# Layer A's score products on TensorE: pairs of fp32 products over 64 rows each, replaced by split fp32r products over 128 rows

## The chip, the cores and the metric

One core of one Trainium2 chip. The metric is the device time of one execution in microseconds (us), as the median of several runs; one more execution is taken by the hardware profiler.

## The reference

The program runs a token mixer block and then two more layers on 256 tokens of width 2048. The change lies in the first of these, layer A, a differential attention with 16 heads. Each head has two components of 64 channels, each with a query and a key that are normalised over those 64 channels, scores with a learned bias and a mask by chunks of 64 tokens, a softmax for each component, and the difference of the two as weights of the values:

```python
def _diff_attention(h, w_in, qk_g, lam_vecs, subln_g, w_out, rel_bias, layer_idx):
    ...
    q = _rmsnorm(q.reshape(B, S, H, 2, d), qk_g[0]) * (d ** -0.5)
    k = _rmsnorm(k.reshape(B, S, H, 2, d), qk_g[1])
    ...
        s = (jnp.einsum('bqhtd,bkhtd->bthqk', qblk, k).astype(jnp.float32)
             + jnp.transpose(bias, (2, 0, 1)).astype(jnp.float32))
        s = jnp.where(_chunk_mask(qpos, kpos), s, NEG_INF)
        p = jax.nn.softmax(s, axis=-1)
        attn = p[:, 0] - lam * p[:, 1]
        return jnp.einsum('bhqk,bkhe->bqhe', attn.astype(v.dtype), v)
```

Queries come in two blocks of 128 tokens; the first block sees 128 keys, the second 256. With 16 heads, 2 components and 2 blocks that makes 64 score products of 64 channels.

## The kernel before

Every large weight matrix is streamed from HBM in tiles of 512 KB. ScalarE (ACT) rounds each to fp32r, the format in which TensorE (PE) takes a product in one pass (`wh_...`), and VectorE (DVE) subtracts to get the rest (`wl_...`); activations are split in the same way, and three fp32r products (hi by hi, lo by hi, hi by lo) stand for one fp32 product. `gemm` does this. Its accumulators are called `acc_...`.

Layer A works in four groups of four heads (`layer_a`, i = 0 to 3). A group has three such gemms of 512 columns, `Aq`, `Ak` and `Av`, each of 96 products with 512 moving columns and eight weight tiles. `qk` normalises what Aq and Ak give, transposes it on PE (`pAq`, `pAk`), and moves it from PSUM to SBUF with one ACTIVATE for two heads (`TAq`, `TAk`: channels of component 0 in partitions 0 to 63, of component 1 in 64 to 127). `attention` then does, per head, the scores (tile `sA`, one PSUM bank per component), bias and minimum on DVE (`eA<-sA,biasA`), exponentials on ACT, the combination of both components on DVE (`eA<-eA,cfA,eA`), three transposes on PE (`ptA`), their eviction (`PTA`) and three products with the values (`poA`). The scores of heads 0 and 1 of a group are put out in one go, component 0 and 1 by turns; those of heads 2 and 3 per component, as banks come free:

```python
for c in range(2):
    cs = slice(64 * c, 64 * c + 64)
    mm(scores[g][c][:, cols], qT[cs, g, qs], kT[cs, g, ks], start=qs.start == 0, stop=True, skip_group_check=True)
```

Nothing is issued in the order of this code. Every operation is recorded (all have line 272, that of the recorder), and a list scheduler (`Plan.schedule`) writes out a fixed order for each engine from prices of its own (`Op.model`), priorities, and the rings of buffers that tiles take in turn (tags `t4`, `t2`, `ps`, `rps` and so on, with their counts in `BUFS`). So while a group's attention goes its way through DVE and ACT, PE does products of the next gemm (Aq of the next group, or Ag after the last) in between. SBUF tiles of 4 KB a partition, `TAq` and `TAk` among them, live in the ring `t4`. At run time the engines only wait for semaphores.

Of the kernel before, what the change touches and what calls it, by code (L numbers as in the profile page):

```python
# [10 lines left out]
F32 = mybir.dt.float32  # L11
F32R = mybir.dt.float32r
AF = mybir.ActivationFunctionType
OP = mybir.AluOpType
AX = mybir.AxisListType

T = 256
# [393 lines left out]
class Kernel:  # L411
# [156 lines left out]
    def run(self):  # L568
        tc, nc, a = self.tc, self.nc, self.a
        with ExitStack() as ctx:  # L570
# [18 lines left out]
            with tc.tile_pool(name="work2", bufs=1, reuse_waits="tile") as work:  # L589
                self.work = nc.pool(work, "work2", 1)  # L590
                self.BUFS = {"t1": 4, "t2": 9, "t15": 8, "t4": 14, "tiny": 24}
                self.layer_a()
                self.layer_b()
                nc.flush(tc)
# [659 lines left out]
    def layer_a(self):  # L1254
        nc, a = self.nc, self.a
# [10 lines left out]
        for i in range(4):  # L1266
            bias = self.sb(f"biasA{i}", [128, 4, 256], "t4")
            nc.sync.dma_start(bias, self.skewed(4 * i, 4))

            G.memset(bias[0:64, :, 0:64], -BIG)  # L1270
            qT = self.qk(f"Aq{i}", x, r, gq[:, 0:1])
            kT = self.qk(f"Ak{i}", x, r, gq[:, 1:2])
            acc = self.gemm(f"Av{i}", x)
            v = self.sb(f"vA{i}", [128, 2, 512], "t4")
            for t in range(2):
                S.activation(v[:, t], acc[t], AF.Identity, scale=r[:, t:t + 1])
            obs.append(self.attention(i, qT, kT, v, bias, nlam))
# [47 lines left out]
    def qk(self, group, x, r, gain):  # L1325
# [4 lines left out]
        out = self.sb(f"T{group}", [128, 4, T], "t4")  # L1330
# [10 lines left out]
        for hp in range(2):  # L1341
# [5 lines left out]
            S.activation(out[:, 2 * hp:2 * hp + 2], p, AF.Identity, scale=gain)  # L1347
        return out

    def attention(self, i, qT, kT, v, bias, nlam):  # L1350
# [5 lines left out]
        scores = {}  # L1356
        for h in range(4):
            n, st = f"{i}{h}", "r" * (h % 2)
            if h % 2 == 0:

                for g in (h, h + 1):
                    scores[g] = [self.ps(f"sA{i}{g}{c}", (128, 384), "r" * (g % 2)) for c in range(2)]
                    for cols, qs, ks in ((slice(0, 128), slice(0, 128), slice(0, 128)), (slice(128, 384), slice(128, 256), slice(0, 256))):
                        for c in range(2):
                            cs = slice(64 * c, 64 * c + 64)
                            mm(scores[g][c][:, cols], qT[cs, g, qs], kT[cs, g, ks], start=qs.start == 0, stop=True, skip_group_check=True)
            mn, sm = self.sb("mnA" + n, [128, 2, 2], "tiny"), self.sb("smA" + n, [128, 2, 2], "tiny")
            es = []
            for c in range(2):
                p = scores[h][c]  # L1370
# [267 lines left out]
```

## Time and profile before

| | |
|---|---|
| Runs | 1516.53 us median of 3 (1515.17 to 1516.99) |
| The profiled execution | 1517.89 us, its span on the core 1516.1 us |
| PE, its weight loads (PEld) | 98%, 88% of the span busy |
| DVE, ACT, POOL | 61%, 49%, 19% |
| DMA | 263.51 MB, all of it on hardware queues and instruction fetch |

The profile gives per instruction a start and a duration. Ends of matmuls are modelled, and matmuls overlap: what a product costs PE is read from one start to the next, not from its duration. A row of the timeline merges instructions of the same kind that follow each other (x16: sixteen records, the shape shown being the first one's), and names at its end what ended the idle time before it. `64*128` is the part of the array that the weights fill (rows by columns); the type shown for TensorE is f32 for fp32 and fp32r alike.

### The profile page before, as it was taken

How to read it: one execution, taken by the hardware profiler on the slowest of the kernel's cores; microseconds unless marked ns; L12 is line 12 of the kernel's file. 1: busy time of each engine (PE TensorE's matmuls, PEld its weight loads, DVE VectorE, ACT ScalarE, POOL GpSimd, SP SyncE). 2: the span in 40 equal slices, each digit the busy share in tenths (PEclk: the TensorE clock that was granted, in tenths of full speed). 3: DMA queues.
4: the chain of work that ended last, by engine and by line, in shares of the span. 5: the costliest groups of instructions: out<-in, count | busy, mean ns of one | idle time of the engine just before them, and what ended most of it. 6: DMA issues, size and time to landing. Idle time of an engine off the chain costs nothing. (4 is left out here: it accounts for less than half of the span.)

```text
span 1516.1 us, 25899 instructions
## 1 busy us (share of the span) xinstructions
PE 1481.7 (98%) x10201; PEld 1326.6 (88%) x10201; DVE 919.7 (61%) x1592; ACT 746.5 (49%) x1223; POOL 288.8 (19%) x390
## 2 busy tenths in 40 slices
PE   9999899899999999999999999999999999999999
PEld 8988789889979988777878787889999998988999
DVE  5875465375756765765656565666564458666544
ACT  6542354344455544756455555555443356455532
POOL 0139843812800000030303021100010001000000
PEclk9999999999999999999999999999999999999999
DMA  9645524444434467664545456556665554555563
GB/s 330 189 133 190 154 78 128 151 136 149 142 97 136 137 213 229 200 210 157 180 159 176 166 174 208 179 180 196 198 207 182 177 173 148 185 203 186 181 209 126
DMA packets 91962, 263.51 MB, mean 174 GB/s; under 512 B 19960, under 2 KB 26512, under 8 KB 91840
## 3 DMA queue, kind: packets, MB, share of 16 engines
q1 hardware_dynamic: 91840, 261.86, 54.2%
q8 instruction: 80, 1.31, 0.4%
q14 instruction: 42, 0.34, 0.1%
HBM read 253.92 MB, written 7.90 MB: 173 GB/s over the span
## 5 line engine op out<-in xcount | busy, mean ns | idle before, releaser
L272 POOL TENSOR_TENSOR blocks<-blocks,bt 32x30 f32<-32x30 f32 (+14 forms) x120 | 85.8, 715 | 9.4
L272 POOL TENSOR_TENSOR bt<-blocks 32x30 f32<-32x30 f32 (+14 forms) x120 | 77.6, 647 | 9.2
L272 PE MATMUL acc_rk<-xh,wh_rk 128*128 128x256 f32 x256 | 73.6, 289 | 1.0 <-ACT wh_rk L272 1.0
L272 PE MATMUL acc_rk<-xh,wl_rk 128*128 128x256 f32 x256 | 73.8, 289 | 0.5 <-DVE wl_rk L272 0.5
L272 PE MATMUL acc_rk<-xl,wh_rk 128*128 128x256 f32 x256 | 73.1, 286 | 0.0
L272 PE MATMUL acc_Ao<-mAh,wl_Ao 128*128 128x256 f32 x256 | 72.7, 284 | 0.0
L272 PE MATMUL acc_Bo<-mBh,wl_Bo 128*128 128x256 f32 x256 | 72.6, 284 | 0.0
L272 PE MATMUL acc_Ao<-mAh,wh_Ao 128*128 128x256 f32 x256 | 72.5, 283 | 0.0
L272 PE MATMUL acc_Ao<-mAl,wh_Ao 128*128 128x256 f32 x256 | 72.4, 283 | 0.0
L272 PE MATMUL acc_Bo<-mBl,wh_Bo 128*128 128x256 f32 x256 | 72.4, 283 | 0.0
L272 PE MATMUL acc_Bo<-mBh,wh_Bo 128*128 128x256 f32 x256 | 72.3, 283 | 0.0
L272 DVE TENSOR_TENSOR wl_Bo<-wr_Bo,wh_Bo 128x1024 fp32r<-128x1024 f32 x32 | 39.2, 1225 | 44.9 <-ACT wh_Bo L272 44.9
L272 DVE TENSOR_TENSOR wl_rk<-wr_rk,wh_rk 128x1024 fp32r<-128x1024 f32 (+1 forms) x33 | 41.2, 1247 | 40.3 <-ACT wh_rk L272 40.3
L272 DVE TENSOR_TENSOR wl_Av<-wr_Av,wh_Av 128x1024 fp32r<-128x1024 f32 x32 | 39.2, 1224 | 41.9 <-ACT wh_Av L272 41.8
L272 DVE TENSOR_TENSOR wl_Ao<-wr_Ao,wh_Ao 128x1024 fp32r<-128x1024 f32 x32 | 41.3, 1292 | 36.2 <-ACT wh_Ao L272 36.2
L272 DVE TENSOR_TENSOR wl_o<-wr_o,wh_o 128x1024 fp32r<-128x1024 f32 x32 | 39.2, 1225 | 38.1 <-ACT wh_o L272 38.1
L272 DVE TENSOR_TENSOR wl_Bg<-wr_Bg,wh_Bg 128x1024 fp32r<-128x1024 f32 x32 | 39.2, 1225 | 34.5 <-ACT wh_Bg L272 34.5
L272 ACT ACTIVATE wh_Bo<-wr_Bo 128x1024 fp32r<-128x1024 f32 x32 | 33.9, 1058 | 53.1 <-PE acc_Bo L272 49.8
L272 DVE TENSOR_TENSOR wl_Ag<-wr_Ag,wh_Ag 128x1024 fp32r<-128x1024 f32 x32 | 39.2, 1225 | 30.6 <-ACT wh_Ag L272 30.5
L272 PE MATMUL acc_Bv<-wl_Bv,xBh 128*128 128x412 f32 (+1 forms) x160 | 56.4, 353 | 1.0 <-DVE wl_Bv L272 1.0
L272 DVE TENSOR_TENSOR wl_Bv<-wr_Bv,wh_Bv 128x824 fp32r<-128x824 f32 (+1 forms) x40 | 40.6, 1019 | 26.8 <-ACT wh_Bv L272 26.6
L272 ACT ACTIVATE wh_rk<-wr_rk 128x1024 fp32r<-128x1024 f32 (+1 forms) x33 | 34.1, 1033 | 45.8 <-PE acc_rk L272 22.9
(764 smaller groups left out, 5376.1 us busy)
## 6 DMA issues: line engine op xcount, KB each, us to landing
wr_o<-w SPq DMA_DIRECT2D x32, 512.0 KB, 4.3
wr_Aq<-w SPq DMA_DIRECT2D x32, 512.0 KB, 3.6
wr_Ak<-w SPq DMA_DIRECT2D x32, 512.0 KB, 3.5
wr_Av<-w SPq DMA_DIRECT2D x32, 512.0 KB, 3.8
wr_Ag<-w SPq DMA_DIRECT2D x32, 512.0 KB, 3.5
wr_Ao<-w SPq DMA_DIRECT2D x32, 512.0 KB, 4.2
wr_Bg<-w SPq DMA_DIRECT2D x32, 512.0 KB, 3.3
wr_Bo<-w SPq DMA_DIRECT2D x32, 512.0 KB, 3.3
```

Source lines behind the costliest of these rows:

```text
L272: op.issued = getattr(getattr(self.nc, op.eng), op.method)(*op.args, **op.kw)
```

## The change

`qk` now stores each component by itself, in fp32r and over all 128 rows. For queries, rows 0 to 63 hold hi and rows 64 to 127 lo. For keys there are two tiles: one with hi in both halves, one with lo in rows 0 to 63 and zeros below. A score is then the sum of two fp32r products over 128 rows: hi by hi plus lo by hi, and hi by lo (with zeros under it). The products of a component stand in a row, and each reads the same 128 weight columns again. Per group ACT has 12 evictions of 64 partitions and 512 elements where it had 4 of 128 partitions, DVE 8 subtractions that it did not have, and POOL two memsets of 64x1024. The ring `t4` goes from 14 to 18 buffers, and `dynamic_dma_scratch_size` is set to 1024 bytes.

```diff
--- before.py
+++ after.py
@@ -588,7 +588,7 @@
                 nc.flush(tc)
             with tc.tile_pool(name="work2", bufs=1, reuse_waits="tile") as work:
                 self.work = nc.pool(work, "work2", 1)
-                self.BUFS = {"t1": 4, "t2": 9, "t15": 8, "t4": 14, "tiny": 24}
+                self.BUFS = {"t1": 4, "t2": 9, "t15": 8, "t4": 18, "tiny": 24}
                 self.layer_a()
                 self.layer_b()
                 nc.flush(tc)
@@ -1268,8 +1268,8 @@
             nc.sync.dma_start(bias, self.skewed(4 * i, 4))
 
             G.memset(bias[0:64, :, 0:64], -BIG)
-            qT = self.qk(f"Aq{i}", x, r, gq[:, 0:1])
-            kT = self.qk(f"Ak{i}", x, r, gq[:, 1:2])
+            qT = self.qk(f"Aq{i}", x, r, gq[:, 0:1], False)
+            kT = self.qk(f"Ak{i}", x, r, gq[:, 1:2], True)
             acc = self.gemm(f"Av{i}", x)
             v = self.sb(f"vA{i}", [128, 2, 512], "t4")
             for t in range(2):
@@ -1322,12 +1322,16 @@
                 blocks[b].append(z[:, 128 * b:128 * b + 128])
         self.split_tokens(mix, k0, blocks, scales)
 
-    def qk(self, group, x, r, gain):
+    def qk(self, group, x, r, gain, keys):
+
 
         nc = self.nc
         V, G, S = nc.vector, nc.gpsimd, nc.scalar
         acc = self.accs.pop(group, None) or self.gemm(group, x)
-        out = self.sb(f"T{group}", [128, 4, T], "t4")
+        out = [[self.sb(f"T{group}{hp}{i}", [128, 2, 2, T], "t4", F32R) for i in range(1 + keys)] for hp in range(2)]
+        if keys:
+            for _, lo in out:
+                G.memset(lo.bitcast(F32)[64:128], 0.0)
         z = [self.sb(f"z{group}{t}", [128, 8, 64], "t2") for t in range(2)]
         ss = self.sb(f"s{group}", [128, 2, 8], "tiny", bufs=None)
         for t in range(2):
@@ -1344,7 +1348,13 @@
                 for t in range(2):
                     h = 2 * hp + j
                     nc.tensor.transpose(p[:, j, t * 128:(t + 1) * 128], z[t][:, 2 * h:2 * h + 2].rearrange("p a b -> p (a b)"), self.ident)
-            S.activation(out[:, 2 * hp:2 * hp + 2], p, AF.Identity, scale=gain)
+            for c in range(2):
+                cs = slice(64 * c, 64 * c + 64)
+                hi, lo = out[hp][0][:, :, c], out[hp][1][0:64, :, c] if keys else out[hp][0][64:128, :, c]
+                S.activation(hi[0:64], p[cs], AF.Identity, scale=gain[cs])
+                if keys:
+                    S.activation(hi[64:128], p[cs], AF.Identity, scale=gain[cs])
+                V.scalar_tensor_tensor(lo, p[cs], gain[0:64], hi.bitcast(F32)[0:64], op0=OP.mult, op1=OP.subtract)
         return out
 
     def attention(self, i, qT, kT, v, bias, nlam):
@@ -1353,21 +1363,16 @@
         mm, tr = nc.tensor.matmul, nc.tensor.transpose
         V, G, S = nc.vector, nc.gpsimd, nc.scalar
         ob = self.sb(f"ob{i}", [128, 2, 512], "t4")
-        scores = {}
         for h in range(4):
             n, st = f"{i}{h}", "r" * (h % 2)
-            if h % 2 == 0:
-
-                for g in (h, h + 1):
-                    scores[g] = [self.ps(f"sA{i}{g}{c}", (128, 384), "r" * (g % 2)) for c in range(2)]
-                    for cols, qs, ks in ((slice(0, 128), slice(0, 128), slice(0, 128)), (slice(128, 384), slice(128, 256), slice(0, 256))):
-                        for c in range(2):
-                            cs = slice(64 * c, 64 * c + 64)
-                            mm(scores[g][c][:, cols], qT[cs, g, qs], kT[cs, g, ks], start=qs.start == 0, stop=True, skip_group_check=True)
             mn, sm = self.sb("mnA" + n, [128, 2, 2], "tiny"), self.sb("smA" + n, [128, 2, 2], "tiny")
             es = []
             for c in range(2):
-                p = scores[h][c]
+                p = self.ps(f"sA{n}{c}", (128, 384), st)
+                q, ks = qT[h // 2][0][:, h % 2, c], [k[:, h % 2, c] for k in kT[h // 2]]
+                for cols, t, m in ((slice(0, 128), 0, 128), (slice(128, 384), 1, 256)):
+                    for j, k in enumerate(ks):
+                        mm(p[:, cols], q[:, 128 * t:128 * t + 128], k[:, 0:m], start=t == j == 0, stop=j == 1, skip_group_check=True)
                 e = self.sb(f"eA{n}{c}", [128, 384], "t15")
                 for t, cols, b in ((0, slice(0, 128), self.keys(bias, h, 128, 128)), (1, slice(128, 384), self.keys(bias, h, 0, 256))):
                     V.tensor_tensor_reduce(e[:, cols], p[:, cols], b, -1.0, 3e38, op0=OP.add, op1=OP.min, accum_out=mn[:, c, t:t + 1])
@@ -1627,7 +1632,7 @@
     import concourse.bacc as bacc
     from concourse.bass_utils import run_bass_kernel_spmd
 
-    nc = bacc.Bacc("TRN2", target_bir_lowering=False, num_devices=1)
+    nc = bacc.Bacc("TRN2", target_bir_lowering=False, num_devices=1, dynamic_dma_scratch_size=1024)
     sent = arrays(inputs)
     a = {n: nc.dram_tensor(n, v.shape, mybir.dt.from_np(v.dtype), kind="ExternalInput").ap() for n, v in sent.items()}
     a["out"] = nc.dram_tensor("out", (D, T), F32, kind="ExternalOutput").ap()
```

The order on PE at the first scores of group 0. Names are sA, group, head, component; TAk and TAq with the group (before) or the group, pair of heads and hi or lo (after). Before:

```order
L272 MATMUL acc_Av0_1_7537<-wh_Av0_14_7560,xAl0_1252 128x512
L272 MATMUL sA000_7564<-TAk0_7526,TAq0_7493 128x128
L272 MATMUL sA001_7565<-TAk0_7526,TAq0_7493 128x128
L272 MATMUL sA000_7564<-TAk0_7526,TAq0_7493 128x256
L272 MATMUL sA001_7565<-TAk0_7526,TAq0_7493 128x256
L272 MATMUL sA010_7566<-TAk0_7526,TAq0_7493 128x128
L272 MATMUL sA011_7567<-TAk0_7526,TAq0_7493 128x128
L272 MATMUL sA010_7566<-TAk0_7526,TAq0_7493 128x256
L272 MATMUL sA011_7567<-TAk0_7526,TAq0_7493 128x256
L272 MATMUL acc_Aq1_0_7614<-wh_Aq1_0_7617,xAh0_1251 128x512
```

And now (head 0; the eight products of head 1 follow in the same way, then the same gemm row):

```order
L272 MATMUL acc_Av0_1_7541<-wh_Av0_14_7564,xAl0_1252 128x512
L272 MATMUL sA000_7570<-TAk000_7527,TAq000_7493 128x128
L272 MATMUL sA000_7570<-TAk001_7528,TAq000_7493 128x128
L272 MATMUL sA000_7570<-TAk000_7527,TAq000_7493 128x256
L272 MATMUL sA000_7570<-TAk001_7528,TAq000_7493 128x256
L272 MATMUL sA001_7572<-TAk000_7527,TAq000_7493 128x128
L272 MATMUL sA001_7572<-TAk001_7528,TAq000_7493 128x128
L272 MATMUL sA001_7572<-TAk000_7527,TAq000_7493 128x256
L272 MATMUL sA001_7572<-TAk001_7528,TAq000_7493 128x256
```

Eight fp32 products of heads 0 and 1, components by turns, have become sixteen, component after component. The later heads have two rows per component before, four now, at nearly the same places among the gemm's products.

On PE, the first transposes (ptA) of head 0 among products of the next gemm. Before, and now:

```order
L272 MATMUL acc_Aq1_1_7615<-wh_Aq1_0_7617,xAh0_1251 128x512
L272 MATMUL acc_Aq1_1_7615<-wl_Aq1_0_7618,xAh0_1251 128x512
L272 MATMUL ptA00_7574<-cst_73,eA000_7570 128x128
L272 MATMUL acc_Aq1_1_7615<-wh_Aq1_0_7617,xAl0_1252 128x512
L272 MATMUL ptA00_7574<-cst_73,eA000_7570 128x128 x2
L272 MATMUL acc_Aq1_0_7614<-wh_Aq1_2_7620,xAh0_1251 128x512
```

```order
L272 MATMUL acc_Aq1_0_7618<-wl_Aq1_2_7625,xAh0_1251 128x512
L272 MATMUL acc_Aq1_0_7618<-wh_Aq1_2_7624,xAl0_1252 128x512
L272 MATMUL ptA00_7576<-cst_73,eA000_7571 128x128
L272 MATMUL acc_Aq1_1_7619<-wh_Aq1_2_7624,xAh0_1251 128x512
L272 MATMUL ptA00_7576<-cst_73,eA000_7571 128x128 x2
L272 MATMUL acc_Aq1_1_7619<-wl_Aq1_2_7625,xAh0_1251 128x512
```

Between the last score of head 1 and the first transpose stood 11 gemm products; now there are 15.

On ACT, the eviction of the keys (TAk<-pAk) among the splits of weight tiles, late in gemm Av of group 0. Before, and now:

```order
L272 ACTIVATE wh_Av0_12_7557<-wr_Av0_12_7556 128x1024
L272 ACTIVATE TAk0_7526<-pAk00_7534,gq_7487 128x512
L272 ACTIVATE TAk0_7526<-pAk01_7535,gq_7487 128x512
L272 ACTIVATE wh_Av0_14_7560<-wr_Av0_14_7559 128x1024
L272 ACTIVATE wh_Aq1_0_7617<-wr_Aq1_0_7616 128x1024
L272 ACTIVATE wh_Aq1_2_7620<-wr_Aq1_2_7619 128x1024
```

```order
L272 ACTIVATE wh_Av0_12_7561<-wr_Av0_12_7560 128x1024
L272 ACTIVATE TAk000_7527<-pAk00_7538,gq_7487 64x2x256 x3
L272 ACTIVATE wh_Av0_14_7564<-wr_Av0_14_7563 128x1024
L272 ACTIVATE TAk000_7527<-pAk00_7538,gq_7487 64x2x256
L272 ACTIVATE TAk010_7529<-pAk01_7539,gq_7487 64x2x256 x2
L272 ACTIVATE wh_Aq1_0_7621<-wr_Aq1_0_7620 128x1024
L272 ACTIVATE TAk010_7529<-pAk01_7539,gq_7487 64x2x256 x2
L272 ACTIVATE wh_Aq1_2_7624<-wr_Aq1_2_7623 128x1024
```

On DVE at the same place, before, and now:

```order
L272 TENSOR_TENSOR wl_Av0_12_7558<-wr_Av0_12_7556,wh_Av0_12_7557 128x1024
L272 TENSOR_TENSOR wl_Av0_14_7561<-wr_Av0_14_7559,wh_Av0_14_7560 128x1024
L272 TENSOR_TENSOR wl_Aq1_0_7618<-wr_Aq1_0_7616,wh_Aq1_0_7617 128x1024
L272 TENSOR_TENSOR wl_Aq1_2_7621<-wr_Aq1_2_7619,wh_Aq1_2_7620 128x1024
L272 ISA eA000_7570,mnA00_7568<-sA000_7564,biasA0_7492 128x128
```

```order
L272 TENSOR_TENSOR wl_Av0_12_7562<-wr_Av0_12_7560,wh_Av0_12_7561 128x1024
L272 SCALAR_TENSOR_TENSOR TAk001_7528<-pAk00_7538,gq_7487,TAk000_7527 64x2x256 x2
L272 TENSOR_TENSOR wl_Av0_14_7565<-wr_Av0_14_7563,wh_Av0_14_7564 128x1024
L272 SCALAR_TENSOR_TENSOR TAk011_7530<-pAk01_7539,gq_7487,TAk010_7529 64x2x256
L272 TENSOR_TENSOR wl_Aq1_0_7622<-wr_Aq1_0_7620,wh_Aq1_0_7621 128x1024
L272 SCALAR_TENSOR_TENSOR TAk011_7530<-pAk01_7539,gq_7487,TAk010_7529 64x2x256
L272 TENSOR_TENSOR wl_Aq1_2_7625<-wr_Aq1_2_7623,wh_Aq1_2_7624 128x1024
L272 ISA eA000_7571,mnA00_7568<-sA000_7570,biasA0_7492 128x128
```

Three evictions stand ahead of the split of the last Av tile (wh_Av0_14) where two did, and two subtractions ahead of its second half (wl_Av0_14) where none did. On POOL the two memsets of a group stand ahead of the squares of its keys (qAk). The order of DMA issues on SP is the same as before, and so is the order of PE outside layer A.

## Rows read from the trace of the kernel before

**Rows 1.** The page: busy time by engine, granted clock by slice, the chain that ended last.

```profile
PE 1481.7 (98%) x10201; PEld 1326.6 (88%) x10201; DVE 919.7 (61%) x1592; ACT 746.5 (49%) x1223; POOL 288.8 (19%) x390
...
PEclk9999999999999999999999999999999999999999
...
PE 36%; DVE 1%; ACT 1%; POOL 0%; DMA 0%; issue 0%; ACTq 0%; DVEq 0%
PE acc_Bo L272 6%; PE acc_Ao L272 6%; PE acc_Ag L272 6%; PE acc_Bg L272 6%; PE acc_Bv L272 5%; PE acc_Bq L272 3%; PE acc_Bk L272 3%; PE pB L272 0%; PE tp L272 0%; PE poB L272 0%; POOL k L272 0%; PE sA L272 0%; DMA wr_Bv<-w 0%; PE poA L272 0%; ACT wh_Bv L272 0%
```

**Rows 2.** One stretch of layer A: us, busy us (instructions) by engine, clock, DMA, GB/s.

```profile
760.00:830.00 70.00, 69.89 (x340) 56.00 (x339) 42.77 (x82) 38.95 (x74) 11.18 (x8) 1.00 0.52 167
```

**Rows 3.** What works on tile sA: records, ns min/median/max, first and last start, forms.

```profile
L272 PE MATMUL sA<-TAk,TAq x128: 269/374/378, 697.4 to 945.9; 64*128 64x128 f32 x64, 64*128 64x256 f32 x64
```

**Rows 4.** Timeline, PE, group 0, first scores: start us, us, engine, what, records.

```profile
697.08 0.39 PE L272 MATMUL acc_Av<-wh_Av,xAl 128*128 128x512 f32 x1
697.40 1.58 PE L272 MATMUL sA<-TAk,TAq 64*128 64x128 f32 x16
698.91 0.50 PE L272 MATMUL acc_Aq<-wh_Aq,xAh 128*128 128x512 f32 x1
...
699.49 0.39 PE L272 MATMUL acc_Aq<-wh_Aq,xAl 128*128 128x512 f32 x1
```

**Rows 5.** Timeline, PE, group 0, a later head: a short run of scores.

```profile
712.08 0.39 PE L272 MATMUL acc_Aq<-wh_Aq,xAh 128*128 128x512 f32 x1
712.40 0.92 PE L272 MATMUL sA<-TAk,TAq 64*128 64x128 f32 x4
713.25 0.50 PE L272 MATMUL acc_Aq<-wl_Aq,xAh 128*128 128x512 f32 x1
...
713.82 0.40 PE L272 MATMUL acc_Aq<-wh_Aq,xAh 128*128 128x512 f32 x1
```

**Rows 6.** Timeline, PE, acc_Bk: first and last of 36 starts, fp32r, 256 columns.

```profile
1199.80 0.28 PE L272 MATMUL acc_Bk<-xBh,wh_Bk 128*128 128x256 f32 x1
...
1204.00 0.28 PE L272 MATMUL acc_Bk<-xBh,wl_Bk 128*128 128x256 f32 x1
```

**Rows 7.** Timeline, PE, pn: eight records of two moving columns, 128-column weights.

```profile
327.04 1.05 PE L272 MATMUL pn<-cst,sq 128*128 128x2 f32 x8
327.96 0.36 PE L272 MATMUL acc_za<-xh,wh_za 128*128 128x256 f32 x1
```

**Rows 8.** Timeline, group 0: transposes of head 0, with what they waited for.

```profile
701.31 0.39 PE L272 MATMUL acc_Aq<-wl_Aq,xAh 128*128 128x512 f32 x1
...
701.80 0.14 PEld L272 LDWEIGHTS ptA<-cst,eA 128*128 128x128 f32 x1 [0.53 <-DVE eA L272]
...
702.71 0.39 PE L272 MATMUL acc_Aq<-wl_Aq,xAh 128*128 128x512 f32 x1
```

**Rows 9.** Timeline, PE, group 0: first and last start around another head's three transposes.

```profile
714.51 0.39 PE L272 MATMUL acc_Aq<-wh_Aq,xAh 128*128 128x512 f32 x1
...
715.77 0.40 PE L272 MATMUL acc_Aq<-wl_Aq,xAh 128*128 128x512 f32 x1
```

**Rows 10.** Timeline, all engines, late acc_Av of group 0.

```profile
687.85 1.27 ACT L272 ACTIVATE TAk<-pAk,gq 128x512 f32<-128x512 f32 x2 [1.09 <-PE pAk L272]
...
689.33 1.06 ACT L272 ACTIVATE wh_Av<-wr_Av 128x1024 fp32r<-128x1024 f32 x1 [0.21 <-PE acc_Av L272]
...
690.42 1.22 DVE L272 TENSOR_TENSOR wl_Av<-wr_Av,wh_Av 128x1024 fp32r<-128x1024 f32 x1 [2.41 <-ACT wh_Av L272]
...
694.59 0.39 PE L272 MATMUL acc_Av<-wh_Av,xAh 128*128 128x512 f32 x1
```

**Rows 11.** Groups on DVE by form: count | busy us, mean ns of one | idle before.

```profile
L272 DVE SCALAR_TENSOR_TENSOR xAl<-tp,par,xAh 128x256 fp32r<-128x256 f32 x12 | 5.7, 479 | 0.8 <-ACT xAT L272 0.7
L272 DVE SCALAR_TENSOR_TENSOR xAl<-tp,par,xAh 128x128 fp32r<-128x128 f32 x8 | 2.7, 347 | 0.1
```

## The prediction, written before the changed kernel ran

> **What bounds the kernel now.** First the page: PE is busy for 98% of the span, the granted clock is in its top tenth in all 40 slices, and the chain that ended last runs through PE and its gemms, with DVE and ACT at 1% each [rows 1]. Then the stretches of layer A: from 760 to 830 us PE is busy for 69.89 of 70 us at clock 1.00 (2.4 GHz), while DVE has 42.77 us of work and ACT 38.95 [rows 2]. So here the time is the sum of what PE's instructions take from one start to the next, as long as nothing that it needs comes late. Next, what works on the score tile: 64 products stand in 128 records, two for each fp32 product [rows 3]. Last, the timeline of PE around the scores, to price them with their surroundings.
>
> A gemm product of 512 columns is the measure there: from 694.59 [rows 10] to 697.08 [rows 4] are 11 starts, 0.226 us each.
>
> **What goes.** In group 0 the sixteen records of heads 0 and 1 stand between two gemm products. From 697.08 to 699.49 are 2.41 us with three gemm starts; less 3 x 0.226 = 0.68 the scores cost 1.73 us [rows 4]. A short run of four records, one component of a later head: 712.08 to 713.82, 1.74 us, again three gemm starts, so 1.06 us [rows 5]. A group has one long run and four short ones, 1.73 + 4 x 1.06 = 5.97 us, and four groups 23.9 us. I take the other three groups at the same price: their forms and counts are the same.
>
> The two kinds of run differ. From the first score to the next gemm product a short run takes 0.85 us [rows 5], the long run 1.51 us for four times the records [rows 4]: its components, in the two halves of the array's rows, run beside each other. In the short runs there is nothing to run beside.
>
> **What comes.** 128 fp32r products over all rows, 64 with 256 moving columns, 64 with 128. 256 columns: from 1199.80 to 1204.00 are 35 intervals, 0.120 us each [rows 6]. An fp32r product with 128 moving columns is not in the trace. From below: 256 columns more cost 0.226 - 0.120 = 0.106 us, so 128 fewer would take 0.053 off, 0.067 us. From above: were it taken in four passes, 4 x 128 columns, it would be as long as 512 columns, 0.226 us. I take 0.115 us, from the row that is nearest in the weights: eight records that each load 128 columns and then stream only two take 327.04 to 327.96, 0.92 us, 0.115 each [rows 7]. Those weights are fp32, but the new products load just as many columns for each record. A group then costs 16 x 0.115 + 16 x 0.120 = 3.76 us, four groups 15.0 us. Saved: 23.9 - 15.0 = **8.8 us**; 11.9 us at 0.067 (a group 2.99), 1.7 us at 0.226 (a group 5.54).
>
> Here a rule speaks against the change. The Trainium skill (TensorEngine Tiling (Array Packing), Key Properties) has tiles of the array work independently, each loading weights and multiplying in parallel; a contraction over 64 rows could so run two by two. By the rule alone every head would cost half a long run, 2 x 1.73 = 3.46 us a group, and the change would lose 4 x 0.30 = 1.2 us. The trace bears it out in the long run and not in the short ones, which hold half the heads at 4.24 us a group; the measured runs decide, and the sum keeps 8.8 us.
>
> **A wait that goes with it.** The first transposes of head 0 wait 0.53 us for DVE's `eA` [rows 8]. From 701.31 to 702.71 are 1.40 us with three gemm starts (0.68), so three transposes took 0.72 us; another head's, not waited for, took 1.26 us less four gemm starts (0.90), 0.36 us [rows 9]. The difference, 0.36 us, occurs once a group: 1.4 us. In the new order 15 gemm products stand ahead of them instead of 11, four more times 0.226 = 0.9 us, and the long run itself costs 16 x 0.1175 = 1.88 us, not 1.73. The chain of DVE and ACT up to `eA` keeps its operations, and the first half of component 0 is now done after two records. So the transposes come about 1 us later relative to a chain that starts no later, and I count the wait as gone. If it stays: 0.
>
> **What lies beside other work.** Per group ACT has 8 more evictions. Two of today's take 1.27 us [rows 10], 0.64 each; with half the partitions, but the same 512 elements in each, I take the same: 5.1 us a group. DVE has 8 more subtractions from PSUM; such an instruction takes 347 ns for 128 columns and 479 for 256 [rows 11], 132 per 128 columns, so 743 ns for 512, 5.9 us a group. In 70 us of layer A, less than a group takes, DVE has 27 us free and ACT 31 [rows 2]: there is room, and what matters is what stands behind it in order. The tightest place is the last tile of Av. Today its first half is split on ACT at 689.33, its second on DVE at 690.42, and its first product starts at 694.59 [rows 10]. Now three evictions stand ahead: 687.85 + 3 x 0.64 = 689.77, the split ends at 690.83; on DVE the subtraction that needs the third eviction ends at 690.5, and the second half runs from about 690.9 to 692.1. That leaves 2.5 us. Behind it the tiles of Aq are split about 1 us later than today, one gemm tile (12 x 0.226 = 2.7 us) or more ahead of need. The keys of heads 0 and 1 are ready by 692, the scores want them at 697.4. So this costs nothing; were that cover gone, each us beyond 2.5 would be paid in all four groups.
>
> Edits at nothing: the memsets on POOL (8 in all, ahead of squares on an engine at 11.18 of 70 us [rows 2]); four more buffers in `t4`; the scratch size. DMA issues keep their order. Past layer A nothing changes its order.
>
> **Sum.** 8.8 + 1.4 = 10.2 us. From the profiled execution's 1517.89 us that gives 1507.7; the median of the runs shown is 1.36 us below it, so for a median 1516.53 - 10.2 = **1506.3 us**.
>
> **Rivals.**
> 1. *The weight load hides.* If 128 columns cost 0.067 us, the saving is 11.9 + 1.4 = 13.3 us, 1503.2. For it: 256 and 512 columns lie on one line with a small offset, so no weight load shows yet at 0.120. Against it: 0.115 with two columns [rows 7]. Chance 0.11. The Trainium skill (TensorE: Matmul & The Clock Gate, Back-to-back issue gap) gives about 81 ns for a sustained pair of weight load and product of 128 columns; by that, an estimate, a group would take 3.22 us and the kernel about 1504.1 us. No row here shows such a pair below 0.115.
> 2. *The change doesn't do what it says.* With 128 moving columns fp32r goes no faster than four passes, 0.226 us: 1.7 + 1.4 = 3.1 us, 1513.4. For it: nothing in the trace has fp32r below 256 columns, and half of the new products are such. Against it: nothing shows a step in the price from 512 to 256. Chance 0.15.
> 3. *The keys come in the way, and it gets slower.* ACT and DVE run in order, and the evictions of `TAk` stand ahead of `wh_Av`, `wl_Av`. If the half-partition forms that move between halves cost k times my prices, the last tile of Av is ready at 687.85 + (3 x 0.64 + 0.74) k + 1.3; it is late beyond k = 2.05 and costs 2.66 (k - 2.05) a group. From k = 3.3 that eats all 10.2 us and 3 more; at k = 4 it is 20.8 us in four groups, 1527.1. For it: neither form is in the trace. Against it: a factor of 3 on a form that keeps its 512 elements per partition. Chance of slower 0.04, of a part of the gain eaten 0.06.
>
> **How the numbers follow.** The forecast has 0.64. About 0.2% (3 us) is what a measurement can tell from no change. Faster by more: the forecast, rival 1, half of the part eaten (0.03) and a third of rival 2, which lies on that bound (0.05), 0.83. Within 0.2%: the rest of rival 2 and of the part eaten, 0.13. Slower: 0.04. The range takes in rival 1 less half the spread of the runs (1503.2 - 0.9 = 1502.3), and upwards the forecast with the wait kept and 0.13 us for each new product (saved 4 x (5.97 - 4.16) = 7.2, 1509.3) plus the whole spread, 1.8: 1511.1. Rival 2 and the slower case, 0.19, lie outside.
>
> **What would show it.** In the new profile: score records one after another about 0.117 us apart, sixteen of them from the last Av product to the first of the next gemm in 2.1 us (1.88 and one gemm start); four in about 0.47 us; no idle "issue" at either end; no DVE wait ahead of head 0's transposes; layer A shorter by 2.5 us a group. Wrong it would be if 128-column records stood 0.22 us apart, or if `acc_Av` or `acc_Aq` waited for `wh` or `wl` behind `TAk`.

## The result, and the profile after the change

The changed kernel takes 1505.56 us (median of 5 runs, 1504.8 to 1510.02), the kernel before 1516.53 (now 5 runs, 1515.17 to 1516.99): a ratio of 0.9938, with an interval of 0.992 to 0.9955. Forecast were 1506.3 us, with 1502.3 to 1511.1 as the range.

The page has the same shape as before [rows 1]: PE is busy for 98% of the span, and DVE and ACT have more to do.

```profile
PE 1471.5 (98%) x10201; PEld 1329.8 (88%) x10201; DVE 942.3 (63%) x1624; ACT 767.8 (51%) x1255; POOL 296.0 (20%) x398
```

The windows view from 760 to 830 us, against [rows 2]: PE has no idle time left, DVE went from 42.77 to 49.07 us and ACT from 38.95 to 46.11. The added work is there, and PE does not feel it.

```profile
760.00:830.00 70.00, 70.00 (x352) 58.84 (x350) 49.07 (x92) 46.11 (x84) 16.58 (x12) 1.00 0.55 174
```

The timeline of PE in group 0 (start, length, operation): the long run, a short run, and head 0's transposes, against [rows 4], [rows 5] and [rows 8].

```profile
695.19 0.39 PE L272 MATMUL acc_Av<-wh_Av,xAl 128*128 128x512 f32 x1
695.42 2.00 PE L272 MATMUL sA<-TAk,TAq 128*128 128x128 f32 x16
697.26 0.40 PE L272 MATMUL acc_Aq<-wh_Aq,xAh 128*128 128x512 f32 x1
...
700.44 0.40 PE L272 MATMUL acc_Aq<-wh_Aq,xAl 128*128 128x512 f32 x1
700.67 0.27 PE L272 MATMUL ptA<-cst,eA 128*128 128x128 f32 x1
700.70 0.48 PE L272 MATMUL acc_Aq<-wh_Aq,xAh 128*128 128x512 f32 x1
701.01 0.38 PE L272 MATMUL ptA<-cst,eA 128*128 128x128 f32 x2
701.15 0.48 PE L272 MATMUL acc_Aq<-wl_Aq,xAh 128*128 128x512 f32 x1
701.47 0.40 PE L272 MATMUL acc_Aq<-wh_Aq,xAl 128*128 128x512 f32 x1
...
704.45 0.39 PE L272 MATMUL acc_Aq<-wl_Aq,xAh 128*128 128x512 f32 x1
704.67 0.62 PE L272 MATMUL sA<-TAk,TAq 128*128 128x128 f32 x4
705.13 0.40 PE L272 MATMUL acc_Aq<-wh_Aq,xAl 128*128 128x512 f32 x1
```

Sixteen products from 695.19 to 697.26: 2.07 us, less one gemm start (0.226) 1.84, or 0.115 each, the mean of eight products with 128 and eight with 256 moving columns. Four from 704.45 to 705.13: 0.68, less 0.226 is 0.45. The first score follows an Av product by 0.23 us, an ordinary distance; before, it was 0.32. The transposes: 700.44 to 701.47, 1.03 less three gemm starts (0.68), 0.35 us, and no wait in brackets.

To compare kernels I use one stretch throughout: from the last Av product of group 0 to the first product of `acc_Ao`, so all scores of layer A and nothing behind it. Before, it runs from 697.08 to 1030.8, **333.7 us**; now from 695.19 to 1019.0, **323.8 us**. That is 9.9 us. What PE's weight loads waited for in it, before (first fence) and now (second; columns: engine, what waited, releaser, us in total, times, longest):

```profile
PEld acc_Aq L272 <- issue: 4.0, 12, 0.3
PEld sA L272 <- issue: 2.9, 8, 0.4
PEld ptA L272 <- DVE eA L272: 2.1, 4, 0.5
PEld sA L272 <- ACT eA L272: 1.5, 4, 0.4
PEld ptA L272 <- issue: 1.3, 4, 0.3
PEld acc_Ag L272 <- issue: 1.3, 4, 0.3
```

```profile
PEld tp L272 <- issue: 0.4, 1, 0.4
```

13.1 us of waits became 0.4. They overlap with PE's work in part, so they aren't all gain. The waits for issue of 0.3 to 0.4 us stand on both sides of the score runs: on entering the 64-row form (`sA`) and on leaving it (`acc_Aq`, `acc_Ag`, `ptA`).

The two profiled executions differ by 12.3 us, 1517.89 to 1505.56. The stretch has 9.9 of it; 1.9 lie ahead, where PE's order is the same in both kernels (697.08 against 695.19 for the same Av product), and 0.5 behind. Whether the 1.9 belong to the change, experiment 7 shows.

### The profile page after: what moved, and what is told of

It is laid out like the page before. It is cut to its first block, busy times and chain, and to the rows that moved or that the text cites. A ratio compares the mean times of both kernels' runs of the same rounds, so it can differ in the third digit from the quotient of the medians.

```text
span 1503.8 us, 25983 instructions
## 1 busy us (share of the span) xinstructions
PE 1471.5 (98%) x10201; PEld 1329.8 (88%) x10201; DVE 942.3 (63%) x1624; ACT 767.8 (51%) x1255; POOL 296.0 (20%) x398
## 4 chain that ended last, share of the span: by engine, by line
PE 86%; POOL 6%; DVE 3%; issue 2%; DMA 1%; ACT 1%; SPq 0%; ACTq 0%; DVEq 0%; POOLq 0%
PE acc_Bo L272 6%; PE acc_Ao L272 6%; PE acc_o L272 6%; PE acc_Ag L272 6%; PE acc_Av L272 6%; PE acc_Aq L272 6%; PE acc_Bg L272 6%; PE acc_Ak L272 5%; PE acc_Bv L272 5%; PE acc_rk L272 3%; PE acc_zb L272 3%; PE acc_q L272 3%; PE acc_Bq L272 3%; PE acc_Bk L272 3%; POOL bt L272 3%; PE acc_v L272 3%
## 5 line engine op out<-in xcount | busy, mean ns | idle before, releaser
L272 POOL TENSOR_TENSOR blocks<-blocks,bt 32x30 f32<-32x30 f32 (+14 forms) x120 | 81.8, 682 | 9.4
L272 POOL TENSOR_TENSOR bt<-blocks 32x30 f32<-32x30 f32 (+14 forms) x120 | 80.8, 674 | 9.2
L272 ACT ACTIVATE wh_Ao<-wr_Ao 128x1024 fp32r<-128x1024 f32 x32 | 33.8, 1057 | 45.5 <-PE acc_Ao L272 38.7
L272 ACT ACTIVATE wh_o<-wr_o 128x1024 fp32r<-128x1024 f32 x32 | 33.9, 1060 | 45.1 <-PE acc_o L272 37.6
```

The costliest lines, as they stand in the source:

```text
L272: op.issued = getattr(getattr(self.nc, op.eng), op.method)(*op.args, **op.kw)
```

## The experiments

All were timed beside the kernel before on their own chip, so each ratio is with that.

**1. The 64-row form alone.** fp32 as before, but over all 128 rows, with zeros in the half of the key tile that the component doesn't use; the ring `t4` and the scratch size are those of the change:

```diff
-        out = self.sb(f"T{group}", [128, 4, T], "t4")
+        out = [self.sb(f"T{group}{c}", [128, 4, T], "t4") for c in range(1 + keys)]
+        if keys:
+            G.memset(out[0][64:128], 0.0)
+            G.memset(out[1][0:64], 0.0)
...
-                            mm(scores[g][c][:, cols], qT[cs, g, qs], kT[cs, g, ks], start=qs.start == 0, stop=True, skip_group_check=True)
+                            mm(scores[g][c][:, cols], qT[0][:, g, qs], kT[c][:, g, ks], start=qs.start == 0, stop=True, skip_group_check=True)
```

> The kernel before, with one key tile per component whose other 64 rows are zero, so that a score is an fp32 product over all 128 rows: four passes as before, no two halves of the array. Theory (the short runs lose their 0.42 us on top of their passes with the 64-row form, the long run loses its overlap): 0.226 us for 128 columns and 0.44 for 256, so a long run 2.66 us instead of 1.73, a short one 0.67 instead of 1.06, a group 5.3 instead of 5.97, four groups 2.6 us less; and the wait of head 0's transposes goes, since the long run is 0.9 us longer: 1.4 us. From the last product of Av in group 0 to the first of Ao (333.7 us before) 329.7; total about 1512.5. Rival (the fixed 0.42 us comes with any run of small products, not with the 64-row form): a group 2.66 + 4 x 0.67 + 5 x 0.42 = 7.4 us, 5.9 us more, total about 1521.

Measured: 1515.14 us (median of 12) against 1518.15, ratio 0.998 (0.9968 to 0.9992). The stretch is 1026.7 - 696.86 = 329.8 us. In it the trace has no wait of PE's loads at all. PE around the long run:

```profile
696.86 0.39 PE L272 MATMUL acc_Av<-wh_Av,xAl 128*128 128x512 f32 x1
697.09 2.78 PE L272 MATMUL sA<-TAk,TAq 128*128 128x128 f32 x16
699.52 0.58 PE L272 MATMUL acc_Aq<-wh_Aq,xAh 128*128 128x512 f32 x1
699.94 0.40 PE L272 MATMUL acc_Aq<-wl_Aq,xAh 128*128 128x512 f32 x1
700.17 0.39 PE L272 MATMUL acc_Aq<-wh_Aq,xAl 128*128 128x512 f32 x1
```

The gemm product behind the run also takes longer than 0.226 us here, so I count three gemm starts, as in [rows 4]: from 696.86 to 700.17 are 3.31 us, less 0.68 is 2.63, 0.165 per record. That is dearer than the 1.73 us of the pairs, since nothing runs beside anything now. A short run, counted in the same way, takes 0.67 us where it took 1.06 (711.28 to 712.63, less three gemm starts). Both are the theory's prices (2.66 and 0.67), and the stretch is 3.9 us shorter, 329.8 against the theory's 329.7. So 2.4 of the 9.9 us come from giving up the 64-row form, its idle ends and its pairs together, with everything still fp32; 1.5 come with the wait of head 0's transposes, which goes here too; the other 6 come with fp32r in place of fp32.

**2. Moving columns.** The changed kernel with 256 moving columns in every score product, 128 of them computed in vain for the first query tile:

```diff
-                for cols, t, m in ((slice(0, 128), 0, 128), (slice(128, 384), 1, 256)):
+                for cols, t, m in ((slice(256, 512), 0, 256), (slice(0, 256), 1, 256)):
```

> The changed kernel, with 256 moving columns in all 128 score products (the first query block takes 128 keys that nothing reads). Theory (a product of 128 moving columns is bound by the load of its 128 weight columns): 64 products go from 0.115 to 0.120 us, 0.3 us more than the changed kernel: from the last Av product to the first of Ao 324.1 us (323.8 there), total about 1506. Rival (the stream sets it, 0.067 us for 128 columns): 64 x 0.053 = 3.4 us more, 327.2 us, about 1509.

Measured: 1507.52 us (6 runs), ratio 0.9934 (0.9915 to 0.9953). The stretch is 1022.6 - 698.08 = 324.5, 0.7 us more than the change. The long run stands between gemm products at 698.08 and 700.22, 2.14 us: (2.14 - 0.226) / 16 = 0.120 each. Only half of its products have changed, so a product with 128 moving columns costs 2 x 0.115 - 0.120 = 0.110 us, and the 128 columns more are worth about 0.01 us (0.7 us over the 64 products), twice the theory's 0.005 and far below the rival's 0.053: the moving side is not what a product takes most of its time from.

**3. Pairs in fp32.** The kernel before, with the scores of heads 2 and 3 also put out for both components by turns, and the transposes `ptA` 0.9 us later in PE's order so that none falls between:

```diff
+        if op.method == "transpose" and op.args[0].tensor.name.startswith("ptA"):
+            return d.end + self.LATENCY[d.eng][op.eng] + self.MARGIN + 900
...
-                            mm(scores[g][c][:, cols], qT[cs, g, qs], kT[cs, g, ks], start=qs.start == 0, stop=True, skip_group_check=True)
+                            op = mm(scores[g][c][:, cols], qT[cs, g, qs], kT[cs, g, ks], start=qs.start == 0, stop=True, skip_group_check=True)
+                            if h == 2:
+                                op.deps[freed[g % 2]] = "data"
```

> The kernel before, fp32 over 64 rows as it was, but the scores of heads 2 and 3 are put out with both components in turns, as those of heads 0 and 1 are (the scheduler is told to wait until both banks are free), and the transposes of the weights are placed 0.9 us later. Theory (components in the two halves of the rows overlap wherever they stand together): a head of a short run costs 1.06 us once, not twice; 2.1 us a group, 8.5 us in all, and 1.4 us for the wait of the transposes: 323.8 us from the last Av product to the first of Ao, total about 1506.6, as the changed kernel. Rival (only the fixed cost is shared, the passes don't overlap): a head 1.28 + 0.42 = 1.70 us, 3.4 us in all and 1.4: 328.9 us, about 1511.7.

Measured: 1509.53 us (6 runs), ratio 0.9941 (0.9925 to 0.9956). The stretch is 326.8 us, between theory and rival. A pair run:

```profile
712.86 0.39 PE L274 MATMUL acc_Aq<-wh_Aq,xAh 128*128 128x512 f32 x1
713.18 0.93 PE L274 MATMUL sA<-TAk,TAq 64*128 64x128 f32 x8
714.04 0.50 PE L274 MATMUL acc_Aq<-wl_Aq,xAh 128*128 128x512 f32 x1
```

Eight records take 0.86 us from the first start to the next gemm product, where four took 0.85 [rows 5]: the second component is free. The waits show where most of the missing 3 us went: `pAq` waits 1.5 us (3 times 0.5) and `tp` 1.5 us for a gate on DVE, neither of which waited before. PE loses less than they sum to: from start to start, `pAq` costs 0.9 us more than before in the three groups together and this `tp` 1.3 us. Experiment 8 goes after that.

**4. The transposes alone.** The kernel before, with only the first two lines of the edit of experiment 3.

> The kernel before, with nothing changed but that the scheduler places the transposes of the weights (ptA) 0.9 us later. Theory (the wait of head 0's transposes was 0.36 us of PE's time in each group): 1.4 us less, 332.3 us from the last Av product to the first of Ao, total about 1515.1. Rival (PE waits elsewhere for the same chain): 333.7 us, about 1516.5.

Measured: 1516.76 us (12 runs), ratio 0.9992 (0.998 to 1.0003). The stretch is 1028.7 - 694.83 = 333.9 us, as before. What PE's loads waited for in it:

```profile
PEld acc_Aq L274 <- issue: 5.0, 15, 0.3
PEld sA L274 <- issue: 2.9, 8, 0.4
PEld acc_Ag L274 <- issue: 1.7, 5, 0.3
PEld pAq L274 <- issue: 1.5, 3, 0.5
PEld sA L274 <- ACT eA L274: 1.5, 4, 0.4
```

The wait of `ptA` for `eA` is gone, all 2.1 us, and the stretch is no shorter. From start to start, over all four groups, the trace shows why. Head 0's transposes take 0.35 us where they took 0.72 (699.96 to 700.99, less three gemm starts), so the 1.4 us are gained. The same edit loses them again elsewhere. About 0.4 go because head 1's transposes no longer stand right behind a short run, where they were nearly hidden: their four waits for issue came back as four more of the gemm (15 and 5 where 12 and 4 were). About 0.9 go at `pAq`, which in the new order waits for DVE's `zAq`:

```profile
741.64 0.39 PE L274 MATMUL acc_Ak<-wl_Ak,xAh 128*128 128x512 f32 x1
742.09 0.41 PE L274 MATMUL pAq<-cst,zAq 128*128 128x128 f32 x2
```

That start comes 0.45 us after the product before it, against 0.24 in the kernel before (742.75 to 742.99). So the rival is right that PE waits elsewhere, but the wait itself was worth what the theory said. No run moved `ptA` and `pAq` together without the pairs.

**5. Half of the products.** The changed kernel with only the first product of each pair:

```diff
-                    for j, k in enumerate(ks):
-                        mm(p[:, cols], q[:, 128 * t:128 * t + 128], k[:, 0:m], start=t == j == 0, stop=j == 1, skip_group_check=True)
+                    mm(p[:, cols], q[:, 128 * t:128 * t + 128], ks[0][:, 0:m], start=t == 0, stop=True, skip_group_check=True)
```

> The changed kernel with the 64 products that have lo of the queries against hi of the keys and hi against lo of the keys left out: only the first of each pair of products (both halves of the queries by hi of the keys) is computed, so lo of the keys does not enter the scores. Keys and queries are prepared as before, the gemms are the same. Theory (each of the new products costs its 0.115 to 0.120 us in PE's order, nothing else hangs on it): from the last Av product of group 0 to the first Ao product 323.8 - 64 x 0.1175 = 316.3 us, and 7.5 us less than the changed kernel run beside it. Rival 1 (a product costs only about 0.08 us where nothing drains): 318.7 us. Rival 2 (the scores' place is taken by waits, since DVE and ACT behind the scores need their time): 320 us or more, with waits of PE for eA, PTA or wh.

Measured: 1499.18 us (4 runs, 1497.67 to 1500.22), ratio 0.9882 (0.9868 to 0.9896); the changed kernel beside it 1507.58, so 8.4 less. The stretch is 1013.7 - 697.11 = 316.6 us, 7.2 less than with both products. A product is worth its 0.113 us in full, and the chain over DVE and ACT follows: the trace has two waits of 0.2 us there. This is the fastest of all, but another computation, with the keys rounded to fp32r in the scores; whoever can accept that can also drop their subtractions and memsets (not run).

**6. The keys twice.** The changed kernel with each key eviction and subtraction done a second time:

```diff
-            for c in range(2):
+            for c in [c for c in range(2) for _ in range(1 + keys)]:
```

> The changed kernel with each key eviction on ACT and each subtraction on DVE done a second time: 8 more evictions of 0.68 us and 4 more subtractions of 0.74 us a group, 5.4 and 3.0 us. Theory (the work that the change added is hidden with little to spare: 1.5 us ahead of the last tile of Av, and the keys of heads 0 and 1 ready about 2 us ahead of their scores): the second four evictions of heads 0 and 1, 2.7 us and turns with DVE, end behind the place of the first scores, and PE waits 1 to 3 us a group for TAk, 4 to 12 us in all: 328 to 336 us between the last Av product of group 0 and the first Ao product. Rival (ACT and DVE have 27 and 31 us free in 70, so the order does not matter): 323.8 us, no wait for TAk.

Measured: 1520.7 us (8 runs), ratio 1.0023 (1.0012 to 1.0034), so slower than the kernel before. The stretch is 1033.8 - 697.27 = 336.5 us, 12.7 over the change and just above the theory's range:

```profile
PEld ptA L272 <- DVE eA L272: 6.9, 5, 2.0
PEld sA L272 <- ACT TAk L272: 3.4, 3, 1.1
PEld sA L272 <- issue: 1.9, 4, 0.6
PEld sA L272 <- ACT ob L272: 1.1, 4, 0.4
PEld sA L272 <- DVE mnA L272: 1.1, 1, 1.1
```

The wait for `TAk` is as the theory had it, in three groups; from start to start, with the other waits of `sA`, the long runs take 6.1 us more than in the change. About as much is lost one step on: the exponentials and `eA` stand behind the second evictions on ACT and DVE, so the transposes wait. The work that the change added is free only as long as it fits ahead of the scores. Eight more evictions and four more subtractions a group (the change added eight and eight) cost more than the change gains, although neither engine is full: in the change DVE has 21 us free in 70 and ACT 24. The theory's "about 2 us ahead" was too little: in the change DVE's last subtraction for heads 0 and 1 starts at 688.89 and takes 0.75 us, and their scores start at 695.42.

**7. The change once more,** with no edit.

> The changed kernel once more, unchanged, beside the others of this call. Theory: 1505 to 1507 us, 10 to 12 us below the kernel before; 323.8 us between the last Av product of group 0 and the first Ao product, within 0.3 us, while what the profiles show ahead of that stretch, where no instruction differs, varies by up to 2 us with the granted clock of the first block. Rival (the 2 us ahead of the stretch belong to the change): that part is again 2 us shorter than in the kernel before.

Measured: 1507.58 us (6 runs, 1504.53 to 1511.84), ratio 0.9944 (0.9929 to 0.9959), 9.3 us below the kernel before (1516.9), just short of the theory's 10 to 12. The profiled execution took 1511.84 us: its last Av product of group 0 comes at 701.46, 6.3 us later than in the first profile of the same kernel, and the stretch is 1025.3 - 701.46 = 323.8 again. So what lies ahead of the stretch varies by 6.3 us for one kernel, more than the 2 us of the theory and the 1.9 us that the first pair of profiles showed there. Nor does it go with the change in the other profiles: that Av product starts at 694.72 to 697.08 in those built on the kernel before, at 694.62 to 701.46 in those built on the change. The 1.9 us need no explanation by the change. The single runs go with the mean granted clock of the whole span: 1504.53 at 0.993, 1511.84 at 0.989.

**8. Pairs, with `pAq` moved as well.**

```diff
-        if op.method == "transpose" and op.args[0].tensor.name.startswith("ptA"):
+        if op.method == "transpose" and op.args[0].tensor.name.startswith(("ptA", "pAq")):
```

> The kernel before with the scores of heads 2 and 3 issued for both components together, as heads 0 and 1 are, and with the transposes ptA and also pAq placed 0.9 us later in PE's order (in the run with pairs before this one pAq waited 1.5 us). Theory (pairs over the two halves of the rows run beside each other, so one group costs 1.73 + 2 x 1.06 = 3.85 us, against 3.76 us for the fp32r products, and the rest was only the place of pAq): 325.3 us between the last Av product of group 0 and the first Ao product, 323.8 us if the one wait of 1.5 us for gA01z goes as well. Rival (the wait moves to the next in order, as it did when only the transposes of the scores came later): 326.8 us or more.

Measured: 1509.87 us (6 runs), ratio 0.9954 (0.994 to 0.9967). The stretch is 1021.2 - 695.27 = 325.9 us, 0.6 over the theory; the waits of `pAq` are gone, and that of `tp` is still there:

```profile
PEld tp L274 <- DVE gA01z L274: 1.5, 1, 1.5
```

The 1.5 us of waits of `pAq` were worth 0.9 us of the stretch (326.8 to 325.9). So the kernel before, merely reordered, gets within 2.1 us of the change in this stretch, 1.3 of which is `tp`, with none of the added work on ACT, DVE and POOL; the intervals of its ratio and of the one in experiment 7 overlap.

**9 and 10. What a product's price is made of.** The changed kernel with four more products ahead of each score tile, with w = 128 and w = 64 weight columns:

```diff
+                for _ in range(4):
+                    mm(p[0:w, 0:128], q[:, 0:w], ks[0][:, 0:128], start=True, stop=True, skip_group_check=True)
                 for cols, t, m in ((slice(0, 128), 0, 128), (slice(128, 384), 1, 256)):
```

> The changed kernel with four more products ahead of the scores of every score tile (128 in all): 128 weight columns of the queries, 128 moving columns of the keys, written to the tile's first 128 columns, which the first score product then overwrites, so that nothing else changes. Theory (0.115 us a product, set by the load of 128 weight columns): 323.8 + 128 x 0.115 = 338.5 us between the last Av product of group 0 and the first Ao product. Rival (a product costs the 0.053 to 0.067 us of its columns once they stand in a row): 331 to 332 us.

> The same with 64 weight columns in each of the 128 additional products, so that they write 64 partitions. Theory (the load of the weight columns sets the price): half of 0.115 us each, and not below the 0.053 us of 128 moving columns: 323.8 + 128 x 0.0575 = 331.2 us. Rival 1 (0.115 us is the price of a record, whatever it loads): 338.5 us, as with 128 weight columns. Rival 2 (a form of tile that uses half of the array's columns makes PE drain on entering and leaving, as the 64-row form does: 0.1 to 0.3 us at each of the two ends of 32 runs, 6 to 19 us): 337 to 350 us, with idle time put down to issue in the waits of PE's loads.

Measured: 1519.77 us (8 runs), ratio 1.0008 (0.9997 to 1.002), and 1519.34 us (8 runs), ratio 1.001 (0.9997 to 1.0023). The whole times don't tell the two apart; the stretches and the long runs do. With 128 weight columns:

```profile
694.62 0.39 PE L272 MATMUL acc_Av<-wh_Av,xAl 128*128 128x512 f32 x1
694.84 3.79 PE L272 MATMUL sA<-TAk,TAq 128*128 128x128 f32 x32
698.47 0.39 PE L272 MATMUL acc_Aq<-wh_Aq,xAh 128*128 128x512 f32 x1
```

3.85 us where the change has 2.07: 1.78 for 16 more, 0.111 each, where experiment 2 gave 0.110. The stretch is 1032.5 - 694.62 = 337.9 us, against 338.5 of the theory. With 64:

```profile
698.23 0.39 PE L272 MATMUL acc_Av<-wh_Av,xAl 128*128 128x512 f32 x1
698.46 3.14 PE L272 MATMUL sA<-TAk,TAq 128*64 128x128 f32 x32
701.44 0.40 PE L272 MATMUL acc_Aq<-wh_Aq,xAh 128*128 128x512 f32 x1
```

3.21 us, 1.14 for 16 more, 0.071 each. So the price falls with the weight columns, though not to half; it isn't a fixed price of a record (rival 1), and no idle time at changes of form shows (rival 2): the short runs, with four more products each, pay 0.072 for a product too, so there is no fixed price at a run's ends. The same products also write 64 partitions in place of 128, which this run doesn't separate from the load; the records that write only two columns at 0.115 us [rows 7] speak for the load. The stretch is 1033.6 - 698.23 = 335.4 us, more than 331.2, and a part of that has a reason of its own:

```profile
PEld ptA L272 <- issue: 3.5, 4, 0.9
```

In PE's timeline this is head 0's first transpose, put down there to DVE's `eA`: DVE did a split of `wl_Aq` between the two components. From start to start head 0's transposes take 1.04 us instead of 0.36, 2.7 us in four groups; without that it would be 332.7 us, by that estimate 0.07 for each of the 128.

## Why the prediction was right, and where it was not

**The price of a product: right, and for the reason given.** The choice of 0.115 us for 128 moving columns came from the row that was nearest in its weights [rows 7], against 0.067 on the line through the moving columns. The long run and experiments 2 and 9 gave 0.110 to 0.111 (its 0.115 is the mean with the products of 256 columns), experiment 2 showed 128 moving columns to be worth about 0.01, experiments 9 and 10 that 64 weight columns less are worth 0.040. Rivals 1 and 2 (0.067 and 0.226) are both out. The Trainium skill (TensorE: Matmul & The Clock Gate, Back-to-back issue gap) has 81 ns a product with 128 columns; the rows show 110 to 115 here, and the measurement decides. The Trainium skill (TensorE: Matmul & The Clock Gate, LDWEIGHTS) gives a weight load a nanosecond for every 1.2 columns, by that, an estimate, 107 ns for 128, which the price of a product comes near, and 53 for 64, which it doesn't reach (71). The trace's own records of the loads overlap and are longer, 192 ns on average for 128 columns and 135 for 64 in experiment 10.

**The scores: 8.8 us predicted, 8.6 measured.** By the prediction's own measure group 0 now costs 1.84 + 4 x 0.45 = 3.64 us (3.76 predicted), so 4 x (5.97 - 3.64) = 9.3. That takes one short run for all. Over the whole stretch, each place counted from the start of the gemm product before it to that of the fourth gemm product behind it, less 0.226 for each gemm product in between, the traces have (us):

| Place, all four groups | Before | Now | Gain |
|---|---|---|---|
| 4 long runs | 6.9 | 7.4 | -0.5 |
| 16 short runs, with `poA` and head 1's transposes beside them | 23.5 | 14.4 | 9.1 |
| head 0's transposes | 2.9 | 1.45 | 1.45 |
| `tp` | 2.8 | 3.1 | -0.2 |
| all other starts | | | 0.1 |

Up to rounding, the gains sum to the stretch's 9.9 us. A short run costs 0.46 to 0.47 us now, a little more than the one at 704.45. Experiment 5 confirms the price of the products over all four groups: 64 products less are 7.2 us, 7.5 expected.

**The transposes: the 1.4 us are there, as predicted.** Head 0's took 0.35 us instead of 0.72, in all four groups, 1.45 us in all, and in the change no other wait took their place but 0.4 us of `tp`, worth 0.2. One thing that the prediction's count missed is visible before the change: the second short run of a group had head 1's transposes right behind it.

```profile
706.73 0.39 PE L272 MATMUL acc_Aq<-wh_Aq,xAl 128*128 128x512 f32 x1
707.04 0.92 PE L272 MATMUL sA<-TAk,TAq 64*128 64x128 f32 x4
707.89 0.33 PE L272 MATMUL ptA<-cst,eA 128*128 128x128 f32 x1
707.98 0.48 PE L272 MATMUL acc_Aq<-wh_Aq,xAh 128*128 128x512 f32 x1
708.29 0.38 PE L272 MATMUL ptA<-cst,eA 128*128 128x128 f32 x2
708.43 0.47 PE L272 MATMUL acc_Aq<-wl_Aq,xAh 128*128 128x512 f32 x1
708.74 0.39 PE L272 MATMUL acc_Aq<-wh_Aq,xAl 128*128 128x512 f32 x1
```

706.73 to 708.74 is 2.01 us, less three gemm starts 1.33, where a short run and three transposes apart cost 1.06 + 0.36 = 1.42. So "four short runs at 1.06" counts 0.09 us a group too much, 0.4 in all; it is why the scores gave 8.6 us and not 9. Experiment 4 loses the same 0.4 us.

**Why the short runs were dear.** The prediction said that they have nothing to run beside. That is half of it. Experiment 3 shows it: with the other component beside it a run costs the same for double the records. Experiment 1 shows the other half: over all rows fp32 gains 2.4 us in the score runs, although each long run loses 0.9 (2.63 against 1.73 us), since each of the 16 short runs gains 0.4 (and head 1's transposes lose their 0.4 here too). What is gained there is the idle time at both ends of the 64-row runs, which the prediction had inside its 1.06 us and named only among its signs (no idle "issue" at either end). The Trainium skill (TensorEngine Tiling (Array Packing), Key Properties) has both: that tiles work independently, and that changing the tiling mode drains the engine. The prediction weighed the first against the change, at 3.46 us a group if every head ran in pairs; the pairs of experiment 3 cost 1.07 us a head in the later heads, not half a long run, so 1.73 + 2 x 1.07 = 3.87 us a group, a little more than the change's 3.64. The second spoke for the change, and the trace agrees for 64 rows, with issue waits of up to 0.3 and 0.4 us at the ends of a run, though not for the 64 columns of experiment 10, where no such wait shows.

**The cover: it held, with 1.5 us instead of 2.5.** ACT and DVE ahead of the last tile of Av, in their timelines (idle before, and its releaser, in brackets):

```profile
687.39 0.74 DVE L272 SCALAR_TENSOR_TENSOR TAk<-pAk,gq,TAk 64x512 fp32r<-64x512 f32 x1 [1.24 <-ACT TAk L272]
688.17 0.68 ACT L272 ACTIVATE TAk<-pAk,gq 64x512 fp32r<-64x512 f32 x1 [0.81 <-DVE TAk L272]
688.88 1.06 ACT L272 ACTIVATE wh_Av<-wr_Av 128x1024 fp32r<-128x1024 f32 x1
...
689.97 1.23 DVE L272 TENSOR_TENSOR wl_Av<-wr_Av,wh_Av 128x1024 fp32r<-128x1024 f32 x1 [0.33 <-ACT wh_Av L272]
```

The prices were right (0.74 us for the subtraction as estimated, 0.68 for an eviction against 0.64). The step that failed is "687.85 + 3 x 0.64 = 689.77": it has the third eviction follow at once, but that waited 0.81 us for DVE's subtraction of the component before. `wl_Av` is done at 691.20, and the first product of that tile, eleven gemm starts ahead of 695.19, starts at 692.70. Experiment 6 shows that rival 3 named a real danger, though not its place: with the key work doubled the kernel is slower than before, but PE waits there for the keys themselves and for `eA`, and has no wait of `acc_Av` or `acc_Aq` for `wh` or `wl`.

**The total:** 10.2 us predicted, 9.9 in the stretch, 11.0 between the medians of the first runs and 9.3 between those of experiment 7. That 1506.3 came within 0.8 us of the first median is in part luck: the medians of the same kernel differ by 2.0 us (1505.56 and 1507.58), and their two profiles differ by 6.3 us ahead of the stretch, where PE's order is that of the kernel before, and by less than 0.1 us in it. The edits priced at nothing (memsets, `t4`, scratch size) were not run by themselves; the sum over the stretch leaves them nothing there.

## What to carry to other kernels

Here a short product's price went with its weight columns far more than with its moving columns: price it by them, and look for that row even if its moving side is quite another. A product on half of the array's rows is cheap only beside its partner on the other half; alone, it pays for the rows that it doesn't use and for the idle time on entering and leaving the form, and putting the partner beside it may win nearly what a rewrite wins. A wait that is removed gives its time back, but the edit that removes it can make another: look at the whole list of waits, and price each from start to start, since less is lost to it than it shows. Compare two kernels over a stretch between the same two instructions rather than over the whole time.

## What the hardware showed that was not expected

- fp32r over 128 rows takes 0.110 us with 128 moving columns and 0.120 with 256 (the change and experiment 2); 64 weight columns in place of 128 bring the former to 0.071 (experiment 10). An fp32 record over 128 rows takes 0.165 on average, half of them with 128 and half with 256 moving columns (experiment 1).
- The tile of 64 weight columns over all rows is entered and left without a wait in the trace (experiment 10); the tile of 64 rows is not, with 0.3 to 0.4 us at an end.
- The same kernel's profiles differ by 6.3 us ahead of layer A's scores and by less than 0.1 us in them.
